# RMSNorm rows by a GpSimd power, a turn in blocks of 32 and a round trip through DRAM, instead of Newton steps and a TensorE broadcast

## The chip, the cores and the metric

The kernel runs on one core of a Trainium2 chip. The metric is device time in microseconds (us) of one execution. Engines: PE is TensorE, DVE is VectorE, ACT is ScalarE, POOL is GpSimd, SP is SyncE, which issues most DMAs. SBUF is the memory on chip with 128 partitions; PSUM, in banks of 128 partitions x 512 numbers, holds what PE sums up.

## The reference

A decoder trunk of two layers on 512 tokens of width 1024, in float32. Layer 0 mixes tokens by multi-head latent attention (MLA), layer 1 by native sparse attention (NSA); each mixer stands between two SwiGLU channel mixers (the ffns) of hidden width 2816. Every one of these six stages starts with an RMSNorm over the width; MLA has two more inside, over the query latent (384) and the key/value latent (256).

```python
def rmsnorm(x, g):
    x32 = x.astype(jnp.float32)
    y = x32 * lax.rsqrt(jnp.mean(x32 * x32, axis=-1, keepdims=True) + RMS_EPS)
    return y.astype(x.dtype) * g

def swiglu(x, w_gate, w_up, w_down):
    return (jax.nn.silu(x @ w_gate) * (x @ w_up)) @ w_down

  h = h + 1/2 * SwiGLU_a(RMSNorm(h))
  h = h + Mixer_i(RMSNorm(h))
  h = h + 1/2 * SwiGLU_b(RMSNorm(h))
```

and one final RMSNorm, which the change does not touch.

## The kernel before

The state h lies in SBUF as eight tiles h0 to h7 of 128 x 512: the width on the partitions, the tokens along the free side. Matrix products run on PE in float32 precision, each as three products of high and low parts (`split` makes the parts: ACT rounds the high part, DVE or POOL subtracts for the low one). Weights come in tile by tile by SP's DMAs and are split in the same way (tiles wr, ru, rg, w, wh, wl).

**A norm is applied late.** The products of a stage run on the tiles of h times the norm's gain, without the factor 1/rms of each token; the results are then multiplied, on DVE, by a tile `row` of 128 x 512 that holds the factor of each token in every partition. So the row is needed only when the first product of a stage leaves PSUM. A row is made in these steps:
1. ACT squares the eight tiles, DVE adds them up (`sumsq`, into s2).
2. `norm_col`: four products of s2 with a column of ones give the sums over the partitions as a column for each block of 128 tokens, a tile `pc` of 128 x 4.
3. `rsqrt` on DVE: v = mean + eps, a first guess by integer operations on the bits (L267, L268), and three Newton steps of three operations (L276, L277, L278), all 128 x 4.
4. `norm_bcast` on PE: four products of the columns, spread over 128, with the identity give `pb`, 128 x 512 in PSUM.
5. ACT copies pb into `row`.

There are seven such rows: in the four ffns (here a0, b0, a1, b1 by layer and place), in MLA for its input (cx) and for the key/value latent (rkv), and in NSA for its input. The query latent's norm in MLA (cq) uses the column alone.

**The head of an ffn.** The hidden width is cut in blocks f of 128. The first two or three blocks are "plain": a product for the gate (pg), a product for the up part (pu), 48 products of 128 x 256 each, with the sums for the norm after block 0 (in a0 the sums come from squares of the tokens, without products). `spread()` then makes the row and applies it: tg<-pg,row (L389), silu, tg<-tg,row (L391), tu<-pu,tg (L400), and the split into ah and al. All later blocks are "fast": seven half-size products (px, pq, pg) of sums of h's quarters and sums of weight quarters. The sums of h are the tiles y, u and four (`combine`), those of the weights s1, rg, ru (`wsums`, L346 to L351), and each weight sum is split into wh and wl ahead of its product.

**MLA's head.** A product pr for the rotary key, then the key/value latent (two tiles pc), the norm cx, the rotary key kr<-pr,row with its small operations (krs on POOL among them), three products for the query latent, the norm rkv, and c<-pc,row (L753), split into four, which the key products pk read.

**NSA's head.** Four products pcm for the compressed keys and values; `layout` multiplies them with the row into tiles xc (L1058, 16 operations); `hidden` is a product ph on xc, a copy posb, a Gelu on ACT; its result hid goes into pkc. `keys(0)` is a product pp (24 matmuls), t<-pp,row and its splits into four; `query` follows.

The program's order on each engine is set by a scheduler from the order of the code; `high_priority(URGENT)` lets what stands inside come earlier. A bank of PSUM or a buffer of a tag is taken again when its last reader is done.

Of the kernel before, what the change touches and what calls it, by code (L numbers as in the profile page):

```python
# [18 lines left out]
P = 128  # L19
S = 512  # L20
# [44 lines left out]
class Kern:  # L65
# [13 lines left out]
    def setup(self):  # L79
# [18 lines left out]
        self.tiny = tiny  # L98

# [160 lines left out]
    def rsqrt(self, y, v, t, psum, n, pool, eps=None):  # L260

        nc = self.nc
        if eps is None:
            nc.vector.tensor_scalar(v, psum, 1.0 / n, EPS, op0=ALU.mult, op1=ALU.add)
        else:
            nc.vector.scalar_tensor_tensor(v, psum, 1.0 / n, eps, op0=ALU.mult, op1=ALU.add)
        nc.vector.tensor_scalar(y.bitcast(I32), v.bitcast(I32), 1, None, op0=ALU.logical_shift_right)  # L267
        nc.vector.tensor_scalar(y.bitcast(I32), y.bitcast(I32), -1.0, float(0x5F3759DF), op0=ALU.mult, op1=ALU.add)  # L268
        for _ in range(3):
            if pool:  # L270
                nc.gpsimd.tensor_tensor(t, y, y, op=ALU.mult)
                nc.gpsimd.tensor_tensor(t, t, v, op=ALU.mult)
                nc.gpsimd.tensor_scalar(t, t, -0.5, 1.5, op0=ALU.mult, op1=ALU.add)
                nc.gpsimd.tensor_tensor(y, y, t, op=ALU.mult)
                continue
            nc.vector.scalar_tensor_tensor(t, y, -0.5, v, op0=ALU.mult, op1=ALU.mult)  # L276
            nc.vector.tensor_tensor(t, t, y, op=ALU.mult)  # L277
            nc.vector.scalar_tensor_tensor(y, t, 1.5, y, op0=ALU.add, op1=ALU.mult)  # L278

    def norm_col(self, n, s2, urgent=0, eps=None):  # L280

        nc = self.nc
        pc = self.bank("o", "pc")
        for i in range(4):
            nc.tensor.matmul(pc[:, i : i + 1], s2[:, i * P : (i + 1) * P], f32v(self.ones)[:, 0:1], start=True, stop=True)
        with self.tc.high_priority(urgent) if urgent else nullcontext():
            return self.rsqrt_col(pc[:, 0:4], n, eps=eps)

    def rsqrt_col(self, s, n, pool=False, eps=None):
        v, t, col = self.vtc[:, 0:4], self.vtc[:, 4:8], self.vtc[:, 8:12]  # L290
        self.rsqrt(col, v, t, s, n, pool, eps)
        return col

    def norm_bcast(self, col):

        pb = self.bank("o", "pb")
        for i in range(4):
            self.nc.tensor.matmul(pb[:, i * P : (i + 1) * P], col[:, i : i + 1].to_broadcast([P, P]), self.ident, start=True, stop=True)
        return pb
# [77 lines left out]
    def ffn(self, idx, gain_next, ap, tp):  # L377
# [63 lines left out]
        def spread():  # L441
            pb = self.norm_bcast(col)
            nc.scalar.activation(row, pb, AF.Copy)
# [4 lines left out]
        row = tp.tile([P, S], F32, tag="row", bufs=1, name="row")  # L448
        gates = [self.bank("T", "pg") for _ in range(plain)]
        for f, g in enumerate(gates):  # L450
            u = tu[f] = self.bank(("mm", "S")[f % 2], "pu")
            self.plain(idx, f, 0, g)
            if f == plain - 1:
                spread()
# [6 lines left out]
            if f == 0 and idx:  # L461
                with self.tc.high_priority(URGENT):
                    for c in self.late:
                        self.sumsq(self.h[c])
                col = self.norm_col(D, self.s2, URGENT)
            elif f == 1 and idx == 0:
                squares(2)
                squares(3)
                col = self.rsqrt_col(sums, D)
# [194 lines left out]
    def mla(self, gain_next):  # L664
        nc, tc, a = self.nc, self.tc, self.a
        with ExitStack() as pools:
# [27 lines left out]
            def rows(col):  # L694
                pb = self.norm_bcast(col)
                t = tp.tile([P, S], F32, tag="o", bufs=12, name="row")
                nc.scalar.activation(t, pb, AF.Copy)
                return t
# [23 lines left out]
            cx = self.norm_col(D, self.s2)  # L722
# [4 lines left out]
            row = rows(cx)  # L727
# [709 lines left out]
```

## Time and profile before

| | |
|---|---|
| time of three runs | 1866.86, 1863.21, 1864.66 us, median 1864.66 |
| span of the profiled execution, first to last instruction | 1860.0 us |
| PE busy | 1841.1 us (99%), 12440 instructions in the trace |
| DVE busy | 1542.0 us (83%), 2862 |
| ACT busy | 1083.9 us (58%), 2044 |
| POOL busy | 232.9 us (13%), 323 |
| granted TensorE clock, mean | 0.999 |
| DMA | 187.44 MB, mean 101 GB/s |

The page gives no time of its own for the profiled execution beside its span; the difference to the runs is what lies before the first instruction and after the last. A row of the timeline gives start, duration, engine, line, operation, output<-input, shapes, count, and in brackets the idle time of the engine just before with what ended it. Rows of PE overlap: what counts is the distance of their starts. A row with a count above one stands for several instructions run together, and a product in float32 is two records of the trace. Lines are those of the kernel before.

### The profile page before, as it was taken

The numbers are of one execution on the slowest core, as the hardware profiler recorded it, in microseconds if no ns is written. First come the engines' busy times: TensorE is split into PE (matmuls) and PEld (weight loads), VectorE is DVE, ScalarE is ACT, GpSimd is POOL, SyncE is SP. The second block draws the span as 40 slices with busy tenths as digits, with TensorE's granted clock in tenths as the row PEclk, the third lists the DMA queues.
The fourth block names the chain that finished last, engine by engine and source line by source line (L and its number), as shares of the span: only waits on it lengthen the run. The fifth ranks groups of instructions, "written<-read, shape, count | busy, mean of one in ns | idle before, by whom it ended". The sixth has DMA issues, their size and how long they took to land. (4 is left out here: it accounts for less than half of the span.)

```text
span 1860.0 us, 32734 instructions
## 1 busy us (share of the span) xinstructions
PE 1841.1 (99%) x12440; PEld 1679.9 (90%) x12440; DVE 1542.0 (83%) x2862; ACT 1083.9 (58%) x2044; POOL 232.9 (13%) x323
## 2 busy tenths in 40 slices
PE   8999999999999999999999999999999999999998
PEld 8999999888889999998999999888888889999997
DVE  8988886688789888887998888765988989988885
ACT  8545554479776554555654545435887866544554
POOL 0000000046500000000000000015666600000000
PEclk9999999999999999999999999999999999999999
DMA  6333333142342333323233332333221124333321
GB/s 245 130 103 102 103 97 115 49 106 72 94 134 94 103 105 112 112 88 115 91 116 110 103 107 87 96 100 97 63 74 63 44 104 131 107 103 106 102 80 67
DMA packets 77901, 187.44 MB, mean 101 GB/s; under 512 B 9632, under 2 KB 37664, under 8 KB 77744
## 3 DMA queue, kind: packets, MB, share of 16 engines
q1 hardware_dynamic: 74640, 180.32, 30.3%
q10 hardware_dynamic: 3104, 5.03, 0.8%
q8 instruction: 98, 1.61, 0.3%
q14 instruction: 59, 0.48, 0.1%
HBM read 178.17 MB, written 2.16 MB: 97 GB/s over the span
## 5 line engine op out<-in xcount | busy, mean ns | idle before, releaser
L167 PE MATMUL pd<-al,wd 128*128 128x512 f32 x576 | 224.1, 389 | 0.0
L168 PE MATMUL pd<-ah,wd 128*128 128x512 f32 x576 | 224.0, 389 | 0.0
L166 PE MATMUL pd<-ah,wd 128*128 128x512 f32 x576 | 224.0, 389 | 0.0
L361 PE MATMUL px<-four,wh 128*128 128x256 f32 x632 | 175.2, 277 | 0.5 <-ACT pg L493 0.5
L363 PE MATMUL px<-four,wl 128*128 128x256 f32 x632 | 174.5, 276 | 0.0
L362 PE MATMUL px<-four,wh 128*128 128x256 f32 x632 | 174.5, 276 | 0.0
L362 PE MATMUL pq<-four,wh 128*128 128x256 f32 x632 | 174.5, 276 | 0.0
L363 PE MATMUL pq<-four,wl 128*128 128x256 f32 x632 | 174.4, 276 | 0.0
L361 PE MATMUL pq<-four,wh 128*128 128x256 f32 x632 | 174.4, 276 | 0.0
L174 ACT ACTIVATE wd<-wdr 128x384 fp32r<-128x384 f32 x192 | 99.2, 519 | 101.5 <-issue 75.5
L175 DVE TENSOR_TENSOR wl<-s,wh 128x512 fp32r<-128x512 f32 x79 | 54.6, 691 | 121.0 <-ACT wh L174 120.9
L413 DVE SCALAR_TENSOR_TENSOR h<-pd,h 128x512 f32<-128x512 f32 x216 | 148.5, 688 | 6.1 <-PE pd L168 6.1
L174 ACT ACTIVATE wh<-s 128x512 fp32r<-128x512 f32 x79 | 49.8, 630 | 136.5 <-PE px L362 131.2
L168 PEld LDWEIGHTS pd<-ah,wd 128*128 128x128 f32 x576 | 108.2, 188 | 22.5
L166 PEld LDWEIGHTS pd<-ah,wd 128*128 128x128 f32 x576 | 108.1, 188 | 19.4
L167 PEld LDWEIGHTS pd<-al,wd 128*128 128x128 f32 x576 | 108.0, 188 | 19.5
L361 PEld LDWEIGHTS px<-four,wh 128*128 128x128 f32 x632 | 118.6, 188 | 1.6 <-ACT pg L493 1.3
L362 PEld LDWEIGHTS px<-four,wh 128*128 128x128 f32 x632 | 118.6, 188 | 0.0
L363 PEld LDWEIGHTS pq<-four,wl 128*128 128x128 f32 x632 | 118.6, 188 | 0.0
L363 PEld LDWEIGHTS px<-four,wl 128*128 128x128 f32 x632 | 118.6, 188 | 0.0
L362 PEld LDWEIGHTS pq<-four,wh 128*128 128x128 f32 x632 | 118.6, 188 | 0.0
L361 PEld LDWEIGHTS pq<-four,wh 128*128 128x128 f32 x632 | 118.6, 188 | 0.0
(367 smaller groups left out, 6037.5 us busy)
## 6 DMA issues: line engine op xcount, KB each, us to landing
wr<-in_w_gu SPq DMA_DIRECT2D x93, 512.0 KB, 3.2
ru<-in_w_gu SPq DMA_DIRECT2D x79, 512.0 KB, 4.2
wdr<-in_w_down SPq DMA_DIRECT2D x192, 192.0 KB, 2.5
wdr<-in_w_down SPq DMA_DIRECT2D x24, 256.0 KB, 2.9
wr<-in_mla_w_o SPq DMA_DIRECT2D x8, 512.0 KB, 3.5
wr<-in_nsa_w_q SPq DMA_DIRECT2D x8, 512.0 KB, 3.5
th<-btab_d SPq DMA_DIRECT2D x16, 256.0 KB, 3.3
wr<-in_nsa_w_o SPq DMA_DIRECT2D x8, 512.0 KB, 3.6
```

The source lines that it names most:

```text
L166: mm(out, wh, xh, start=first, stop=False)
L167: mm(out, wh, xl, start=False, stop=False)
L168: return mm(out, wl, xh, start=False, stop=last)
L174: nc.scalar.activation(hi, src, AF.Copy)
L175: (nc.gpsimd if pool else nc.vector).tensor_tensor(lo, src, f32v(hi), op=ALU.subtract)
L361: mm(out, wh[:, p], xh, start=first and p == 0, stop=False, skip_group_check=True)
L362: mm(out, wh[:, p], xl, start=False, stop=False, skip_group_check=True)
L363: mm(out, wl[:, p], xh, start=False, stop=last and p == KP - 1, skip_group_check=True)
L413: nc.vector.scalar_tensor_tensor(self.h[c], p, 0.5, self.h[c], op0=ALU.mult, op1=ALU.add)
```

## The change

For the seven rows and the cq column, the root is one POOL operation, a power of -0.5 (a constant column `root` is its second operand). For a row it is written into the columns 0, 32, 64, 96 of the row tile, whose first 128 columns POOL has cleared. DVE turns that 128 x 128 in blocks of 32, so that the factors of 32 tokens at a time lie along the free side in partitions 0, 32, 64, 96. A DMA on POOL's queue writes these 16 pieces of 128 bytes to a tile `nrow` in DRAM, and a second one, when the first has landed, reads the 512 numbers into all 128 partitions of the row. The products pb and ACT's copy are gone. In NSA the column stays where it was, since it is used later, and DVE copies it into the row.

Three moves come with it. In ffn b0, a1 and b1 the products for the sums stand between the gate and the up product of block 0, not behind the up product. In MLA `rows` makes column and row in one go: cx's row is started right behind the first latent product, and rkv's ahead of `query_latent(1)`. In NSA the first five pieces of `keys(0)` stand ahead of `hidden(0)`, instead of three behind it.

```diff
+        self.root = self.gains[:, 62:63]
+        nc.gpsimd.memset(self.root, -0.5)
...
-    def rsqrt(self, y, v, t, psum, n, pool, eps=None):
...
-        nc.vector.tensor_scalar(y.bitcast(I32), v.bitcast(I32), 1, None, op0=ALU.logical_shift_right)
-        nc.vector.tensor_scalar(y.bitcast(I32), y.bitcast(I32), -1.0, float(0x5F3759DF), op0=ALU.mult, op1=ALU.add)
-        for _ in range(3):
...
-            nc.vector.scalar_tensor_tensor(t, y, -0.5, v, op0=ALU.mult, op1=ALU.mult)
-            nc.vector.tensor_tensor(t, t, y, op=ALU.mult)
-            nc.vector.scalar_tensor_tensor(y, t, 1.5, y, op0=ALU.add, op1=ALU.mult)
...
+    def rsqrt_col(self, s, n, urgent=0, eps=None, col=None):
+
+        nc, v = self.nc, self.vtc[:, 0:4]
+        col = self.vtc[:, 8:12] if col is None else col
+        with self.urgent(urgent):
...
+                nc.vector.tensor_scalar(v, s, 1.0 / n, EPS, op0=ALU.mult, op1=ALU.add)
...
+        nc.gpsimd.tensor_tensor(col, v, self.root.to_broadcast([P, 4]), op=ALU.pow)
         return col
 
-    def norm_bcast(self, col):
-
-        pb = self.bank("o", "pb")
-        for i in range(4):
-            self.nc.tensor.matmul(pb[:, i * P : (i + 1) * P], col[:, i : i + 1].to_broadcast([P, P]), self.ident, start=True, stop=True)
-        return pb
+    def norm_row(self, row, urgent=0):
+
+        nc = self.nc
+        d = self.dp.tile([4, P], F32, name="nrow")[:, :]
+        with self.urgent(urgent):
+            nc.vector.transpose(row[:, P : 2 * P], row[:, 0:P])
+        nc.gpsimd.dma_start(bass.AP(tensor=d.tensor, offset=d.offset, ap=[[32, 4], [P, 4], [1, 32]]),
+                            row[0:P:32, P : 2 * P].rearrange("g (b c) -> g b c", c=32))
+        nc.gpsimd.dma_start(row, bass.AP(tensor=d.tensor, offset=d.offset, ap=[[0, P], [1, S]]))
+
+    def row_tile(self, pool, **kw):
+        row = pool.tile([P, S], F32, name="row", **kw)
+        self.nc.gpsimd.memset(row[:, 0:P], 0.0)
+        return row
...
         def spread():
-            pb = self.norm_bcast(col)
-            nc.scalar.activation(row, pb, AF.Copy)
...
             self.plain(idx, f, 0, g)
+            if f == 0 and idx:
+                with self.tc.high_priority(URGENT):
+                    for c in self.late:
+                        self.sumsq(self.h[c])
+                self.norm_col(D, self.s2, URGENT, col=row[:, 0:P:32])
+                self.norm_row(row, URGENT)
...
             self.plain(idx, f, 1, u)
-            if f == 0 and idx:
...
-                col = self.norm_col(D, self.s2, URGENT)
-            elif f == 1 and idx == 0:
+            if f == 1 and idx == 0:
                 squares(2)
                 squares(3)
-                col = self.rsqrt_col(sums, D)
+                self.rsqrt_col(sums, D, col=row[:, 0:P:32])
+                self.norm_row(row)
...
-            def rows(col):
-                pb = self.norm_bcast(col)
-                t = tp.tile([P, S], F32, tag="o", bufs=12, name="row")
-                nc.scalar.activation(t, pb, AF.Copy)
+            def rows(n, s2, eps=None):
+                t = self.row_tile(tp, tag="o", bufs=12)
+                self.norm_col(n, s2, URGENT, eps, t[:, 0:P:32])
+                self.norm_row(t, URGENT)
                 return t
...
             ps = [self.proj(a["mla_w_in"][0], P, xh, xl, "pc")]
-            cx = self.norm_col(D, self.s2)
+            row = rows(D, self.s2)
...
             ps.append(self.proj(a["mla_w_in"][1], P, xh, xl, "pc"))
-            row = rows(cx)
...
             query_latent(0)
-            rkv = self.norm_col(KVL, sums[0], eps=eps)
+            rkv = rows(KVL, sums[0], eps)
             query_latent(1)
-            rkv = rows(rkv)
...
                 col = self.norm_col(D, self.s2)
-                nc.scalar.activation(row, self.norm_bcast(col), AF.Copy)
+                nc.vector.tensor_copy(row[:, 0:P:32], col)
+                self.norm_row(row)
                 xc = layout(0, ps)
                 ps = tokens(1)
+                kf = keys(0)
+                for f in kf[:5]:
+                    f()
                 hid, w2 = hidden(0, xc)
-                kf = keys(0)
-                for f in kf[:3]:
-                    f()
```

In the program's order this looks as follows; line numbers of the new kernel are a few lower or higher for the same statement (L389 is L388 there, L175 is L177).

DVE in the head of ffn b0, before: the last Newton step, and what leads to tg<-pg,row and on to the low part of the weight sum rg.

```order
L175 TENSOR_TENSOR wl_6640<-ru_6631,wh_6639 128x1024
L277 TENSOR_TENSOR small_76<-small_76 128x4
L175 TENSOR_TENSOR four_6624<-u_6618,four_6624 128x1024
L278 SCALAR_TENSOR_TENSOR small_76<-small_76 128x4
L351 TENSOR_TENSOR rg_6629<-rg_6629 128x512
L175 TENSOR_TENSOR w_6762<-wr_6757,w_6762 128x1024
L347 TENSOR_TENSOR s1_6761<-ru_6759 128x512
L389 TENSOR_TENSOR tg_6534<-pg_6322,row_6321 128x512
L389 TENSOR_TENSOR tg_6597<-pg_6323,row_6321 128x512
L175 TENSOR_TENSOR wl_6646<-rg_6629,wh_6645 128x1024
```

And with the change, from v to the first tg<-pg,row:

```order
L279 TENSOR_SCALAR small_76<-pc_6343 128x4
L177 TENSOR_TENSOR four_6414<-u_6408,four_6414 128x1024
L290 STREAM_TRANSPOSE row_6279<-row_6279 128x128
L244 TENSOR_TENSOR u_6418<-y_6417,u_6418 128x256
L151 TENSOR_TENSOR w_6429<-wr_6428,w_6429 128x1024
L151 TENSOR_TENSOR w_6492<-wr_6491,w_6492 128x1024
L177 TENSOR_TENSOR four_6424<-u_6418,four_6424 128x1024
L242 TENSOR_TENSOR u_6555<-y_6554 128x512
L242 TENSOR_TENSOR u_6565<-y_6564 128x512
L243 TENSOR_TENSOR u_6555<-y_6554,u_6555 128x256
L388 TENSOR_TENSOR tg_6481<-pg_6281,row_6279 128x512
```

The whole head of the norm has moved ahead of the later sums of h, and with it tg<-pg,row and what follows from it: tg<-tg,row, tu and al of both plain blocks now stand ahead of the low part of rg.

DVE in MLA's head, before, from the last steps of cx to the first operation of rkv's norm:

```order
L277 TENSOR_TENSOR small_76<-small_76 128x4
L278 SCALAR_TENSOR_TENSOR small_76<-small_76 128x4
L258 TENSOR_TENSOR s2_4120<-s2_4120,sq_4159 128x512
L731 TENSOR_TENSOR kr_4162<-pr_4054,row_4157 128x512
L149 TENSOR_TENSOR w_4277<-wr_4276,w_4277 128x1024
L737 TENSOR_TENSOR kr_4162<-kr_4162,kr2_4168 64x512
L266 SCALAR_TENSOR_TENSOR small_76<-pc_4215,small_76 128x4
```

With the change, from cx's v to rkv's turn:

```order
L279 TENSOR_SCALAR small_76<-pc_4093 128x4
L722 TENSOR_SCALAR small_76<-small_76 128x4
L290 STREAM_TRANSPOSE row_4091<-row_4091 128x128
L151 TENSOR_TENSOR w_4208<-wr_4207,w_4208 128x1024
L729 TENSOR_TENSOR kr_4141<-pr_4044,row_4091 128x512
L260 TENSOR_TENSOR s2_4106<-s2_4106,sq_4138 128x512
L735 TENSOR_TENSOR kr_4141<-kr_4141,kr2_4147 64x512
L151 TENSOR_TENSOR w_4245<-wr_4244,w_4245 128x1024
L740 TENSOR_TENSOR kr_4141<-kr_4141,crot_4143 64x512
L742 TENSOR_TENSOR krs_4150<-kr_4141,krs_4150 64x512
L281 SCALAR_TENSOR_TENSOR small_76<-pc_4196,small_76 128x4
L290 STREAM_TRANSPOSE row_4194<-row_4194 128x128
```

One split of a weight stands between cx's turn and kr<-pr,row, and rkv's v has moved behind the whole rotary key.

POOL in the same place, with the change (before, it had only krs and the splits w here):

```order
L297 MEMSET row_4194 128x128
L739 TENSOR_TENSOR krs_4150<-krs_4150,crot_4144 64x512
L282 TENSOR_TENSOR row_4194<-small_76,gains_77 128x4
L291 DMA nrow_4203<-row_4194 4x4x32
L155 TENSOR_TENSOR w_4296<-wr_4295,w_4296 128x512
L293 DMA row_4194<-nrow_4203 128x512
```

The split of a weight (w, 128 x 512) stands between the write and the read of rkv's row.

DVE in NSA's head, before, around the second half of xc and up to the copy posb that the Gelu waits for:

```order
L1058 TENSOR_TENSOR xc_14357<-pcm_14258,row_14123 64x32x8 x4
L149 TENSOR_TENSOR w_14422<-wr_14421,w_14422 128x1024
L1058 TENSOR_TENSOR xc_14357<-pcm_14288,row_14123 64x32x8 x4
L149 TENSOR_TENSOR w_14458<-wr_14457,w_14458 128x1024
L1069 COPY posb_14332<-ph_14315 128x1
```

And with the change:

```order
L1055 TENSOR_TENSOR xc_14297<-pcm_14184,row_14059 64x32x8 x4
L151 TENSOR_TENSOR w_14348<-wr_14347,w_14348 128x1024
L1055 TENSOR_TENSOR xc_14297<-pcm_14214,row_14059 64x32x8 x4
L151 TENSOR_TENSOR w_14384<-wr_14383,w_14384 128x1024
L972 TENSOR_TENSOR t_14269<-pp_14244,row_14059 128x512
L151 TENSOR_TENSOR w_14425<-wr_14424,w_14425 128x912
L980 TENSOR_TENSOR four_14061<-t_14269,four_14061 64x512
L981 TENSOR_TENSOR four_14061<-t_14269,four_14061 64x512
L980 TENSOR_TENSOR four_14061<-t_14269,four_14061 64x512
L1066 COPY posb_14290<-ph_14273 128x1
```

The product pp of `keys(0)` runs on PE ahead of ph now, and t<-pp,row with three of its four low parts stands ahead of posb. On PE pkc has moved behind the first ten of the second ph's sixteen products.

More of the change, by code (lines that the diff above doesn't have):

```diff
@@ L258, in sumsq, with norm_col @@
             nc.vector.tensor_tensor(self.s2, self.s2, sq, op=ALU.add)
-    def rsqrt(self, y, v, t, psum, n, pool, eps=None):
[L262 to L266, printed above, removed]
-        nc.vector.tensor_scalar(y.bitcast(I32), v.bitcast(I32), 1, None, op0=ALU.logical_shift_right)
-        nc.vector.tensor_scalar(y.bitcast(I32), y.bitcast(I32), -1.0, float(0x5F3759DF), op0=ALU.mult, op1=ALU.add)
-        for _ in range(3):
[L270 to L275, printed above, removed]
-            nc.vector.scalar_tensor_tensor(t, y, -0.5, v, op0=ALU.mult, op1=ALU.mult)
-            nc.vector.tensor_tensor(t, t, y, op=ALU.mult)
-            nc.vector.scalar_tensor_tensor(y, t, 1.5, y, op0=ALU.add, op1=ALU.mult)
-    def norm_col(self, n, s2, urgent=0, eps=None):
+    def norm_col(self, n, s2, urgent=0, eps=None, col=None):
         nc = self.nc
@@ L285, in norm_col, with urgent @@
             nc.tensor.matmul(pc[:, i : i + 1], s2[:, i * P : (i + 1) * P], f32v(self.ones)[:, 0:1], start=True, stop=True)
[L286 to L291, printed above, removed]
-        return col
-    def norm_bcast(self, col):
-        pb = self.bank("o", "pb")
-        for i in range(4):
-            self.nc.tensor.matmul(pb[:, i * P : (i + 1) * P], col[:, i : i + 1].to_broadcast([P, P]), self.ident, start=True, stop=True)
-        return pb
+        return self.rsqrt_col(pc[:, 0:4], n, urgent, eps, col)
+    def urgent(self, n):
+        return self.tc.high_priority(n) if n else nullcontext()
+    def rsqrt_col(self, s, n, urgent=0, eps=None, col=None):
+        nc, v = self.nc, self.vtc[:, 0:4]
+        col = self.vtc[:, 8:12] if col is None else col
+        with self.urgent(urgent):
+            if eps is None:
+                nc.vector.tensor_scalar(v, s, 1.0 / n, EPS, op0=ALU.mult, op1=ALU.add)
+            else:
+                nc.vector.scalar_tensor_tensor(v, s, 1.0 / n, eps, op0=ALU.mult, op1=ALU.add)
+        nc.gpsimd.tensor_tensor(col, v, self.root.to_broadcast([P, 4]), op=ALU.pow)
+        return col
+    def norm_row(self, row, urgent=0):
[10 more added lines that the diff above has]
+        return row
     def proj(self, src, m, xh, xl, name, w=None):
@@ L446, in spread @@
                 act(e)
-        row = tp.tile([P, S], F32, tag="row", bufs=1, name="row")
+        row = self.row_tile(tp, tag="row", bufs=1)
         gates = [self.bank("T", "pg") for _ in range(plain)]
@@ L945, in nsa @@
             nc.gpsimd.memset(f32v(kc), 0.0)
-            row = mp.tile([P, S], F32, name="row")
+            row = self.row_tile(mp)
             xh, xl = self.xh, self.xl
@@ L1091, in nsa @@
                 self.split(pk[:, : G * 32].rearrange("p (g n) -> p g n", g=G), at(kch), at(kcl))
-                for f in kf[3:]:
+                for f in kf[5:]:
                     f()
```

3 lines of the change are left out of this document (removed).

## The prediction

> **What bounds the kernel now.** I read the page's first part (busy time), then who PE waits for, and then the timeline of each engine around the eight norms.
>
> ```profile
> PE 1841.1 (99%) x12440; PEld 1679.9 (90%) x12440; DVE 1542.0 (83%) x2862; ACT 1083.9 (58%) x2044; POOL 232.9 (13%) x323
> ```
>
> TensorE (PE) is busy 99% of a span of 1860.0 us. Only two things shorten this kernel: work taken off PE, and the few stretches in which PE waits. POOL is nearly idle. The broadcast that is removed is work on PE, and it costs this much:
>
> ```profile
> 359.62 1.05 PE L298 MATMUL pb<-ident,small 128*128 128x128 f32 x8
> 360.43 0.48 PE L166 MATMUL pc<-x,w 128*128 128x512 f32 x1
> 566.64 1.13 PE L298 MATMUL pb<-ident,small 128*128 128x128 f32 x8 [0.34 <-DVE small L278]
> 567.52 0.36 PE L375 MATMUL pu<-x,w 128*128 128x256 f32 x1
> PE pb L298 <- DVE small L278: 1.0, 3, 0.4
> 395.56 0.44 PE L166 MATMUL s<-four 128*128 128x384 f32 x1 [0.64 <-DVE small L661]
> ```
>
> Start to start, the four products pb hold PE 0.81 us in MLA and 0.88 us in ffn b0. Seven of them make about 6.0 us. The waits ahead of pb for the last Newton step (L278) are 1.0 us in three places (total, count, longest), and the wait for the first softmax, which stands behind the Newton steps of the cq norm on VectorE (DVE), is 0.64 us. So the ceiling of the whole change is 6.0 + 1.0 + 0.6 = 7.6 us, 0.4% of the time.
>
> **What the new path costs.** v goes to POOL for the power, back to DVE for the turn in blocks of 32, to POOL's queue for the write, and, when that has landed, for the read. The power is 128x4; the nearest POOL row is the small one below, so 0.2 us, and I take 0.4 with the hand-overs (bounds 0.2 and the 1.34 us of POOL's 128x512). The turn is 128x128 on DVE; its neighbours are the 128x4 rows of 0.16 us and the 128x256 rows of 0.42 (both quoted with the heads below), the bounds, and I take 0.3 between them. With v's own 0.16 and a hand-over the turn ends v + 0.95 us when DVE is free.
>
> ```profile
> L920 POOL TENSOR_SCALAR btab<-tb 16x2 f32<-16x2 f32 x1 | 0.2, 185 | 0.0
> L153 POOL TENSOR_TENSOR w<-wr,w 128x512 fp32r<-128x512 f32 x43 | 56.8, 1340 | 56.7 <-ACT w L147 56.3
> four<-in_g_fin ACTq DMA_DIRECT2D x2, 256.0 KB, 3.3
> rot<-in_c_rope ACTq DMA_DIRECT2D x2, 256.0 KB, 2.6
> tb<-in_rel_bias ACTq DMA_DIRECT2D x1, 2.0 KB, 1.5
> btab_d<-btab ACTq DMA_DIRECT2D x1, 65.0 KB, 4.7
> pos<-in_nsa_pos ACTq DMA_DIRECT2D x2, 8.0 KB, 4.9
> ```
>
> The trace has no DMA of POOL's queue, so the time L from the end of the turn to the landed row is bounded. The read has a twin: four<-in_g_fin spreads one row of 512 numbers over 128 partitions, 3.3 us from issue to landing. It could be as short as rot's 2.6 or as long as the 4.9 of pos. The write is 2 KB: 1.5 us as tb, the same bytes the other way, or 4.7 as btab_d, a write of 65 KB; I take 2.2, near tb by size, more because it writes to DRAM. With 0.5 for two issues and hand-overs L is 2.2 + 3.3 + 0.5 = 6.0 us, from 4.1 to 9.6. L decides the sign, as follows.
>
> **The four ffn heads.** In b0, a1 and b1 the sums move ahead of the up product of block 0, 48 products sooner, and v with them. The row, used at 568.90 before, would land near 559. But tg<-pg,row also moves forward on DVE: behind the turn stand only one L244, two L151, one L177, two L242 and one L243 before it.
>
> ```profile
> 552.85 1.22 DVE L175 TENSOR_TENSOR four<-u,four 128x1024 fp32r<-128x1024 f32 x1
> 553.99 0.42 DVE L242 TENSOR_TENSOR u<-y,u 128x256 f32<-128x256 f32 x1
> 554.32 1.22 DVE L149 TENSOR_TENSOR w<-wr,w 128x1024 fp32r<-128x1024 f32 x1
> 555.46 0.69 DVE L240 TENSOR_TENSOR u<-y 128x512 f32<-128x512 f32 x1
> 556.06 1.22 DVE L175 TENSOR_TENSOR four<-u,four 128x1024 fp32r<-128x1024 f32 x1
> 557.53 0.16 DVE L264 TENSOR_SCALAR small<-pc 128x4 f32<-128x4 f32 x1
> 568.90 1.29 DVE L389 TENSOR_TENSOR tg<-pg,row 128x512 f32<-128x512 f32 x2
> 570.11 1.22 DVE L175 TENSOR_TENSOR wl<-rg,wh 128x1024 fp32r<-128x1024 f32 x1
> 569.80 0.28 PE L361 MATMUL px<-x,w 128*128 128x256 f32 x1
> 571.16 0.28 PE L361 MATMUL pq<-four,wh 128*128 128x256 f32 x1
> 572.78 0.28 PE L363 MATMUL px<-four,wl 128*128 128x256 f32 x1
> ```
>
> The first five rows follow each other without a gap, so DVE is full here, and they give the prices start to start: 1.14 us for 1024 columns, 0.60 for 512, 0.33 for 256. PE's products of 256 columns go one in 0.113 us (twelve between the first two PE rows), so the 48 are 5.4 us. The work before tg is 3 x 1.14 + 2 x 0.60 + 2 x 0.33 = 5.3 us. At L = 6.0 DVE stands 0.7 us at tg, and all its list behind it shifts. That list feeds PE: the low part wl<-rg, done before at 571.33, for the px at 572.78. In the new order two tg*row, two tu and two al come ahead of it, 6 x 0.60 = 3.6 us; one s1 goes behind it (-0.6); eleven tiny operations of 0.16 like the L264 row vanish, of which I count half, since neighbours overlap (bounds 0 and 1.8), -0.9; the turn adds 0.25. It ends at 571.33 + 2.35 + 0.7 = 574.4. On PE fifteen more products of 0.11 stand before that px now, while pb and its gap are gone: 572.78 + 1.7 - 0.9 - 0.3 = 573.3. PE waits 1.1 us where it saved 1.2: net -0.1. Each us of L is a us here, down to -0.8 at L = 5.3, where the wait at tg is gone. I take -0.1 for a1 and b1 too, whose heads are alike, and for a0, whose sums stay but whose tg stands 5.7 us behind the turn. Four heads: -0.4. The POOL clearing of the row's first columns has no producer and costs nothing while POOL is idle.
>
> **MLA.**
>
> ```profile
> 354.27 0.16 DVE L264 TENSOR_SCALAR small<-pc 128x4 f32<-128x4 f32 x1 [3.92 <-PE pc L285]
> 361.34 0.69 DVE L731 TENSOR_TENSOR kr<-pr,row 128x512 f32<-128x512 f32 x1 [0.20 <-ACT row L697]
> 366.97 0.16 DVE L266 SCALAR_TENSOR_TENSOR small<-pc,small 128x4 f32<-128x4 f32 x1 [2.82 <-PE pc L285]
> 367.96 1.76 POOL L153 TENSOR_TENSOR w<-wr,w 128x512 fp32r<-128x512 f32 x1 [1.15 <-ACT w L147]
> 374.54 1.28 DVE L753 TENSOR_TENSOR c<-pc,row 128x512 f32<-128x512 f32 x2
> 376.02 1.42 DVE L178 SCALAR_TENSOR_TENSOR four<-c,gains,four 128x512 fp32r<-128x512 f32 x2 [0.20 <-ACT four L177]
> 378.81 0.39 PE L166 MATMUL pk<-four,w 128*128 128x512 f32 x1
> ```
>
> The first row lands at 354.27 + 0.95 + 6.0 = 361.2, as it did (kr at 361.34). The sum for rkv comes 0.8 sooner with one pb gone, v near 366.2, the second row near 373.3 with POOL's own delay, and c (row L753, 374.54 before) about 1.2 sooner, so four ends near 376.2 instead of 377.44. PE reaches the keys' first pk at 378.81 - 1.6 = 377.2. The two pbs are gained whole, and I add half of the 0.64 at the first softmax: -1.9. POOL's 128x512 w stands between write and read of the second row, 1.76 us, beside the write. Beyond L = 6.4 both rows delay the keys, the second waiting for DVE's kr list behind the first: 2 us for each us of L.
>
> **NSA.** Here the column is wanted again later, so it is copied into the row first (one more DVE operation, 0.2, and the turn at v + 1.3).
>
> ```profile
> 1228.76 0.16 DVE L264 TENSOR_SCALAR small<-pc 128x4 f32<-128x4 f32 x1 [1.41 <-PE pc L285]
> 1234.07 7.66 DVE L1058 TENSOR_TENSOR xc<-pcm,row 64x256 f32<-64x256 f32 x12 [1.94 <-ACT row L1080]
> 1243.01 2.55 DVE L1058 TENSOR_TENSOR xc<-pcm,row 64x256 f32<-64x256 f32 x4
> 1242.04 1.28 ACT L1073 ACT_TABLE_LOAD   x1
> 1251.67 0.61 ACT L981 ACTIVATE four<-t 64x512 fp32r<-64x512 f32 x1
> 1247.51 0.46 PE L1089 MATMUL pkc<-hid,w 128*128 128x128 f32 x2 [0.24 <-issue]
> 1250.55 3.74 PE L1067 MATMUL ph<-xc,w 128*128 128x129 f32 x32
> 1254.04 0.48 PE L166 MATMUL pp<-x,w 128*128 128x512 f32 x1
> ```
>
> DVE already idles 1.94 us for the row and starts xc at 1234.07. The new row lands at 1228.76 + 1.3 + 6.0 = 1236.1, 2.0 later, and xc is one solid list. The reorder puts t<-pp and the hi/lo splits ahead of posb and hid. From the row: sixteen xc 10.2, two w 2.4, t 0.7, four splits on ACT 2.5, the table load 1.3, hid and hand-over 0.6, so pkc can run 17.7 us after the row, at 1253.8. Behind pkc PE keeps only six ph (sixteen in 1250.55 to 1254.04, so 1.3 in all) and pkc's own 0.2; it would reach pkc at 1254.04 - 1.5 - 0.9 (pb) - 0.2 (the gap ahead of pkc) = 1251.4, and waits 2.4. Net 2.4 - 0.9 - 0.2 = +1.3, a us for a us of L.
>
> **The sum** at L = 6.0 is -0.4 - 1.9 + 1.3 = -1.0 us. The profiled execution spans 1860.0 and the median of the three runs is 1864.66, so 4.7 us lie around the span (the runs spread from 1863.21 to 1866.86). 1859.0 + 4.7 gives 1863.7. The slope is 5 us for each us of L up to 6.4 and 7 beyond.
>
> **The rivals.** *Faster, 0.34: the landings are short.* Below L = 5.5, between tb's 1.5 + rot's 2.6 = 4.1 and my value, the waits at tg vanish: heads 4 x -0.8, MLA -1.9, NSA about 0 gives -5.1 and 1859.6; the ceiling, 7.6, gives 1857.1. For it speaks that tb's size and pieces are those of the write. Against it: the only write in the trace took 4.7. [...]
>
> *Slower, 0.28: POOL's three steps (power, two issues) each wait for a running DVE operation.* In the heads DVE has no gap, and its operations last up to 1.22 us; POOL's 128x512 rows average 1.34 us, and the one quoted in MLA lasted 1.76. Three waits of half such an operation add 1.8 and make L 7.8: 0.4 x 5 + 1.4 x 7 = 11.8 over my sum, 1875.5. It decides from L = 6.8, where the loss passes 3.7 us; the place where it bites first is the keys in MLA. A write as long as btab_d's would do the same. [...]
>
> *Same within 0.2%, 0.38: L between 5.5 and 6.8*, 1861 to 1868. 0.2%, or 3.7 us, is about what this measurement can tell from no change. In this case belongs that the heads gain nothing because DVE's list, not the row, is what PE waits for.
>
> The forecast is the middle case. The range takes in the short landings nearly to the ceiling and the long ones to L = 7.4 (-1.0 + 2 + 7 = +8): 1857.5 to 1872. Cases of both signs hold most of the chance; the middle one's own range is 1861 to 1868.
>
> **What would show it.** No pb, no row copy on ACT, and PE busy about 6 us less. The two nrow DMAs' landings add up to 5.5 us without issue. In b0 DVE stops below 1 us at tg for the row's DMA; px<-four waits about 1 us for wl. In MLA pk has no wait. In NSA DVE waits at xc about 4 us, and pkc waits 2 to 3 us. I am wrong if a write or read lands after 4 us or more, if POOL's power takes above 1 us, or if tg is reached late enough to hide all of L.

## The result, and the profile after

The changed kernel takes 1887.81 us (median of 4 runs, 1885.33 to 1889.96) against 1864.1 us before: 1.0128 times as long, 95% interval 1.0116 to 1.0141, or 23.7 us slower. The forecast was 1863.7, in a range of 1857.5 to 1872.0.

The profiled execution spans 1888.1 us against 1860.0, so it is 28.1 us longer, more than the 23.7 of the medians: at 1889.96 us it lies 2.2 above the median of its kernel. Numbers by place below are from it. Its busy times, its new DMA queue, and whom PE waits for (line, releaser, total us, times, longest):

```profile
PE 1851.2 (98%) x12384; PEld 1684.7 (89%) x12384; DVE 1536.5 (81%) x2782; ACT 1080.8 (57%) x2037; POOL 253.7 (13%) x353
q0 software_dynamic: 784, 1.85, 0.3%
PE pq L362 <- DVE wl L177: 5.4, 3, 2.4
PE pkc L1087 <- issue: 3.8, 1, 3.8
PE pk L168 <- ACT four L179: 2.8, 1, 2.8
PE pu L374 <- DVE w L151: 1.7, 1, 1.7
```

PE has 56 records fewer, the seven broadcasts, and is busy 10 us more. Part of the answer stands in the granted clock, the share of full speed that the trace records for TensorE. These are windows of 16 and 24 us in MLA's keys and ffn b0, of before and then of the changed kernel (busy us of PE, of the weight load, DVE, ACT and POOL, each with its count; then the granted clock, the DMA share, GB/s):

```profile
376.00:392.00 16.00, 16.00 (x77) 13.35 (x76) 11.42 (x22) 9.82 (x18) 6.02 (x5) 1.00 0.35 98
572.00:596.00 24.00, 24.00 (x182) 22.81 (x182) 24.00 (x38) 14.86 (x26) 0.00 (x0) 1.00 0.35 119
```
```profile
376.00:392.00 16.00, 13.24 (x45) 10.04 (x44) 10.65 (x12) 6.89 (x12) 4.08 (x5) 0.79 0.42 116
572.00:596.00 24.00, 20.65 (x145) 19.50 (x145) 21.15 (x31) 12.16 (x20) 0.00 (x0) 0.86 0.19 66
```

After the waits the clock is at half for a while. The trace's clock record has four such stretches inside the changed program, 6.83, 6.83, 3.41 and 6.83 us (MLA, b0, NSA, b1), and none before. In MLA it looks like this on PE's timeline:

```profile
384.06 0.79 PE L168 MATMUL pk<-four,w 128*128 128x512 f32 x1 [2.75 <-ACT four L179]
386.71 0.63 PE L170 MATMUL pk<-four,w 128*128 128x512 f32 x1
387.14 0.63 PE L168 MATMUL pk<-four,w 128*128 128x512 f32 x1
```

The products start 0.43 us apart, where the same shape starts every 0.23 us at full clock in the trace of before (378.81, 379.04).

The chain of a row, on POOL and in the list of DMAs (KB and us to landing), in a0, MLA and b0, and then on DVE, in b0, a0 and NSA:

```profile
31.50 0.59 POOL L293 DMA_DIRECT2D row<-nrow  x1 [3.77 <-DMA nrow<-row]
358.88 1.05 POOL L282 TENSOR_TENSOR row<-small,gains 128x4 f32<-128x4 f32 x1 [10.25 <-DVE small L279]
360.58 0.64 POOL L291 DMA_DIRECT2D nrow<-row  x1 [0.64 <-DVE row L290]
362.88 0.57 POOL L293 DMA_DIRECT2D row<-nrow  x1 [1.66 <-DMA nrow<-row]
559.63 1.87 POOL L282 TENSOR_TENSOR row<-small,gains 128x4 f32<-128x4 f32 x1 [29.74 <-DVE small L279]
nrow<-row POOLq DMA_DIRECT2D x7, 2.0 KB, 1.7
row<-nrow POOLq DMA_DIRECT2D x7, 256.0 KB, 4.2
```
```profile
559.32 0.16 DVE L279 TENSOR_SCALAR small<-pc 128x4 f32<-128x4 f32 x1
561.54 0.31 DVE L290 STREAM_TRANSPOSE row<-row 128x128 f32<-128x128 f32 x1 [0.93 <-POOL row L282]
569.64 0.69 DVE L388 TENSOR_TENSOR tg<-pg,row 128x512 f32<-128x512 f32 x1 [2.54 <-DMA row<-nrow]
590.16 1.23 DVE L177 TENSOR_TENSOR wl<-ru,wh 128x1024 fp32r<-128x1024 f32 x1 [1.86 <-ACT wh L176]
593.06 0.69 DVE L388 TENSOR_TENSOR tg<-pg,row 128x512 f32<-128x512 f32 x1 [0.99 <-PE pg L362]
35.70 1.29 DVE L388 TENSOR_TENSOR tg<-pg,row 128x512 f32<-128x512 f32 x2 [3.90 <-DMA row<-nrow]
1252.53 0.63 DVE L1055 TENSOR_TENSOR xc<-pcm,row 64x256 f32<-64x256 f32 x1 [5.46 <-DMA row<-nrow]
```

The power takes 1.05 to 1.9 us. From the end of the turn it is 0.3 us to the write's issue, 1.7 to 1.8 to its landing (4.0 in a0), 0.5 to 0.7 to the read's issue and 4.2 (3.6 to 5.2) to the landed row: 6.8 in all with the middle values, 9.1 in a0, and in b0 10.3 us from v to tg (559.32 to 569.64). DVE, which had no gap in b0's head before, stands 0.93, 2.54, 1.86 and 0.99 us.

What TensorE waits for in b0 is not the row itself but the low part of a weight sum, wl<-ru, which the products pq read. Before, it was done 6 us ahead of them, and ahead of both tg; now it stands behind two tg<-pg,row, two tg<-tg,row, one tu and one al, and every stand of DVE ahead of it delays it. DVE and PE, before and then with the change:

```profile
563.99 1.22 DVE L175 TENSOR_TENSOR wl<-ru,wh 128x1024 fp32r<-128x1024 f32 x1
571.38 0.28 PE L363 MATMUL pq<-four,wl 128*128 128x256 f32 x1
```
```profile
578.26 1.22 DVE L177 TENSOR_TENSOR wl<-ru,wh 128x1024 fp32r<-128x1024 f32 x1
579.53 0.39 PE L362 MATMUL pq<-four,wl 128*128 128x256 f32 x1 [2.22 <-DVE wl L177]
```

Where the loss lies, from equal PE products in the two traces: a0 +4.2, MLA +3.0, b0 +6.2, a1 +1.5, NSA +4.5, b1 +8.3, 27.7 us in all. Such distances are given by place for the other kernels too.

### The profile page after: what moved, and what is told of

It reads as the page before. It is cut to its first block, busy times and chain, and to the rows that moved or that the text cites. A ratio compares the mean times of both kernels' runs of the same rounds, so it can differ in the third digit from the quotient of the medians.

```text
span 1888.1 us, 32584 instructions
## 1 busy us (share of the span) xinstructions
PE 1851.2 (98%) x12384; PEld 1684.7 (89%) x12384; DVE 1536.5 (81%) x2782; ACT 1080.8 (57%) x2037; POOL 253.7 (13%) x353
## 5 line engine op out<-in xcount | busy, mean ns | idle before, releaser
L177 DVE TENSOR_TENSOR wl<-s,wh 128x512 fp32r<-128x512 f32 x79 | 54.5, 689 | 119.3 <-ACT wh L176 119.3
```

Source lines behind the costliest of these rows:

```text
L177: (nc.gpsimd if pool else nc.vector).tensor_tensor(lo, src, f32v(hi), op=ALU.subtract)
```

## The experiments

The first theory was lateness: the row comes too late, and the clock makes each wait dearer. Its rival was order: the moves put the norm's work ahead of what TensorE needs.

**The power alone**, in place of the root from bits and three Newton steps on DVE.

```diff
-        nc.vector.tensor_scalar(y.bitcast(I32), v.bitcast(I32), 1, None, op0=ALU.logical_shift_right)
...
+        nc.gpsimd.tensor_tensor(y, v, self.root.to_broadcast([P, 4]), op=ALU.pow)
```

> The kernel before with one change: the root by GpSimd's power in place of the bit operations and Newton steps; broadcast by TensorE, row copy by ACT and all places as before. Latency theory (the loss of the changed kernel comes from the time from v to the landed row, and from the TensorE clock that halves after the waits): the power takes 1.05 to 1.9 us in the trace of the changed kernel, the eleven small DVE operations it replaces took 2.2 us back to back and 9 us in the full heads, so the waits ahead of pb (1.0 us) and part of that ahead of the first softmax (0.6) go: 1 to 2 us faster, 1862.5 to 1863.7. Rival, the power itself is what hurts (POOL in the chain, locked out by DVE): slower by 2 us or more, with longer waits ahead of pb.

1864.87 us, ratio 1.0007 (0.9999 to 1.0016): no change. MLA is 1.0 ahead, b0 0.9, but NSA 1.4 behind: its broadcast waits 1.9 us for the power. The small gain that was expected is not there, and neither is harm of 2 us or more from the power by itself.

**The moves alone**, with Newton roots, broadcast and row copy: the sums half a block sooner, and in NSA five keys ahead of hidden(0), where three stood behind it.

```diff
             self.plain(idx, f, 0, g)
+            if f == 0 and idx:
...
+                col = self.norm_col(D, self.s2, URGENT)
...
-                hid, w2 = hidden(0, xc)
...
-                for f in kf[:3]:
+                for f in kf[:5]:
...
+                hid, w2 = hidden(0, xc)
```

> The kernel before with the moves alone: the sums of ffn b0, a1, b1 ahead of block 0's up product, and five pieces of keys(0) ahead of hidden(0) in NSA; roots, broadcast and row copy as before. Latency theory: the row is there sooner, nothing waits for it, so 1862 to 1866, no half clock inside the program. Rival, the order does it (tg, tu and al ahead of the low parts that TensorE needs, posb behind the key splits): the waits for wl in b0, a1, b1 and for pkc stay, slower by 8 to 20 us, 1873 to 1885.

1863.8 us, ratio 1.0001 (0.9992 to 1.001). The moves by themselves cost nothing. DVE's list is not that of the changed kernel here, since the Newton steps stand in it; the next run has that list.

**Rows without lateness.** The row is loaded early from 512 numbers of a weight, so the norm's factor is left out of the results; the power, a turn and a small write go on beside it.

```diff
+        g = self.a["w_last"]
+        self.nc.gpsimd.dma_start(row, bass.AP(tensor=g.tensor, offset=g.offset, ap=[[0, P], [1, S]]))
```

> The changed kernel with all its moves, but the row tile is loaded early from 512 numbers of a weight, so that nothing waits for the norm; the power, a turn of 128x32 and a write of 4 pieces go on beside it without a reader, and the norm's factor is left out of the results. Latency theory: all waits of the changed kernel go and the seven broadcasts are gone, 5 to 8 us faster than before, 1857 to 1860, and the clock is never halved inside the program. Rival, the order does it: the waits for wl and pkc stay, 1870 or more.

1863.62 us, ratio 1.0001 (0.9992 to 1.001). In b0 the same twenty operations stand between the turn and wl<-ru as in the changed kernel, so it is not their order that costs: lateness is the loss. But the forecast gain of 5 to 8 us is not there either. By place: MLA -3.0 and NSA -1.7, where broadcasts really were on the path; b0 +1.2, a1 +0.3, b1 +0.9; a0 +3.1. What a0 loses here lies in the first 20 us and belongs to the stand-in: the first products wait 1.6 us for a tile of h, whose loads land after 7.1 us (median) beside the first row load instead of 4.9, and the clock reaches full speed at 14.8 us instead of 10.0. The places without a0 add up to 2.3 us ahead. With free rows the heads of b0, a1 and b1 gain nothing from the missing broadcasts. In b0 DVE is full but for 0.94 us, in which it still stands for the power ahead of the turn, and PE's one longer wait, 1.4 us at px, is for a copy of ACT's that stands behind ACT's split of rg, the last of DVE's sums.

**Idle products in PE's waits**, in the heads ahead of the last product of pq, in MLA ahead of the keys, in NSA ahead of pkc.

```diff
+                self.fill(10)
             self.product(7, w, q, True, False)
...
+            self.fill(12)
...
+                self.fill(26)
```

> The changed kernel with idle TensorE work where TensorE waits: products of the identity with itself that nobody reads, 12 ahead of the keys in MLA, 10 ahead of the first pq of the low parts in ffn b0 and b1, 26 ahead of pkc in NSA, 58 in all, 11.7 us at the 0.2 us of a broadcast product. If the halved clock after a wait is a cost of its own: the fill takes the place of the waits, the four windows of half clock (6.8, 6.8, 3.4 and 6.8 us in the changed kernel's trace, half of which is lost) go, and the kernel is 8 to 12 us faster than the changed one, 1876 to 1880, with more work. If the clock is a bystander, the time stays that of the changed kernel, 1887, or grows by what the fill doesn't hide, to 1892.

1888.92 us, ratio 1.0136 (1.0122 to 1.015): no gain over the changed kernel, where 8 to 12 us were expected. By place MLA went from +3.0 to +0.05, as expected: its fill took the wait, and the clock stayed at full in the window of MLA's keys,

```profile
376.00:392.00 16.00, 15.85 (x86) 13.44 (x85) 13.61 (x16) 9.37 (x17) 6.95 (x8) 1.00 0.42 118
```

but b0 stayed at +6.1 and b1 at +8.1: PE got through its fill and waited 1.7 and 1.7 us at the next two products for wh and wl instead. In NSA the fill pushed the second ph behind pkc, +4.9.

**More fill in b0 and b1**, 14 products more ahead of the px that waits next, none in NSA.

> The changed kernel with idle TensorE products at more of its waits: 12 ahead of the keys in MLA; in ffn b0 and b1 10 ahead of the first pq of the low parts and 14 ahead of the px that waits for wh and wl after it. NSA has none. The first fill took the half clock out of MLA (3.0 us gained in the trace there) but left b0 and b1 where they were, since there the wait only moved on to px. If the halved clock is a cost of its own: MLA is at +0, b0 and b1 at +3 to +4 instead of +6.2 and +8.3 in the trace, 6 to 9 us less than the changed kernel, 1879 to 1882. If in the heads DVE's list sets the end and TensorE's clock is a bystander there: MLA alone gains, 1885 to 1888.

1889.65 us, ratio 1.0139 (1.0122 to 1.0156), a little above the 1885 to 1888 of the second case. MLA -0.1; b0 +7.5 and b1 +7.8, without any stretch of half clock in either. So the full clock alone did not bring the heads back. What the half clock costs there this run can't tell, since the fill is itself longer (4.9 us) than the waits that it fills (3.3).

**The same DMAs from another queue.**

```diff
-        nc.gpsimd.dma_start(row, bass.AP(tensor=d.tensor, offset=d.offset, ap=[[0, P], [1, S]]))
+        nc.scalar.dma_start(row, bass.AP(tensor=d.tensor, offset=d.offset, ap=[[0, P], [1, S]]))
```

The write is moved likewise; in the second kernel both stand on `nc.sync`.

> The changed kernel, its two DMAs of each row issued on ACT's queue. In the changed kernel a row took, from the end of the turn, 0.3 us to the issue, 1.75 to the write's landing, 0.5 to the read's issue and 4.2 to its landing, 6.8 in all. Theory, POOL's queue makes the round trip long: the read lands in 3.3 us as the same spread does from ACT's queue before the change and the hand-overs shrink, 5.5 us in all; 1.3 us less in each of seven rows, and fewer half-clock windows, 6 to 12 us faster than the changed kernel: 1876 to 1882. Rival, the trip is as long from any queue: 1886 to 1890, or more, since ACT's work behind the waiting DMAs (four, y, wh) is late too.

> As the one before, on SP's queue, where no work of ACT stands behind the waits, only weight loads. Theory, POOL's queue makes it long: 1874 to 1882. Rival, the trip is as long from any queue: 1886 to 1890; if weight loads that stand ahead wait for buffers, the rows are later still, above 1890.

From ACT's queue 1870.36 us, ratio 1.0039 (1.0025 to 1.0053); from SP's 1874.47, ratio 1.0056 (1.0041 to 1.0071). So up to 17 of the 24 us went with POOL's queue, more than expected. The trip from turn to use is 5.2 to 6.5 us outside a0 on both queues. In b0 DVE's timeline reads, on ACT's queue and then on SP's,

```profile
554.09 0.31 DVE L290 STREAM_TRANSPOSE row<-row 128x128 f32<-128x128 f32 x1 [0.93 <-POOL row L282]
560.83 0.69 DVE L388 TENSOR_TENSOR tg<-pg,row 128x512 f32<-128x512 f32 x1 [0.57 <-DMA row<-nrow]
552.03 0.31 DVE L290 STREAM_TRANSPOSE row<-row 128x128 f32<-128x128 f32 x1 [0.92 <-POOL row L282]
558.60 0.69 DVE L388 TENSOR_TENSOR tg<-pg,row 128x512 f32<-128x512 f32 x1 [0.33 <-DMA row<-nrow]
```

1.4 us less of trip took 2.0 us from DVE's wait at tg and 4.4 us from b0 (+6.2 to +1.8); the halved clock is gone with it, and of the later stands of 1.86 and 0.99 us one of 0.43 is left. On ACT's queue the scheduler has also put wl<-ru ahead of tg<-tg,row, so that run changes two things. SP's run changes one: the same twenty operations stand ahead of wl<-ru as in the changed kernel, the trip is 1.5 us shorter, and b0 is at +1.5. MLA is at -2.15 on ACT's queue and -1.9 on SP's, a gain at last. On SP's queue NSA is at +6.7: its pkc waited 5.2 us.

**MLA and NSA alone**, heads with power and broadcast, POOL's queue.

> The changed path in MLA (two rows) and NSA (one row); the four ffn heads with the sums where they were, the root by power, the broadcast by TensorE and ACT's copy. By place the changed kernel's trace is later than before by 4.2 us in a0, 3.0 in MLA, 6.2 in b0, 1.5 in a1, 4.5 in NSA and 8.3 in b1. If the places add up: about 7.5 us slower than before, 1869 to 1873, so that two thirds of the loss lie in the heads. Rival, the loss is that of MLA and NSA and spreads (buffers, weight loads): 1880 or more.

1870.52 us, ratio 1.004 (1.0026 to 1.0054), inside the 1869 to 1873 that were expected if the places add up. The profiled execution is the fastest of the five, 1867.57 us, and in it MLA alone is not as expected: it is at +0.2, with a wait of 2.1 us at pk and no half clock, against +3.0 with 2.75 us and 6.8 us of half clock in the changed kernel. The wait itself only gives back what the broadcasts had cost; of the 2.8 us between the two, 0.6 is the longer wait, and the rest is within the 3.4 us, half of 6.8, that this half clock can cost by estimate.

**The pieces on an idle chip.**

> None of the trunk: only the pieces of the new path on an idle chip, one after the other. A power of 128x4 on POOL and, for comparison, a product of 128x4, each four times alone, beside a DVE operation with two SBUF inputs (128x1024), beside one with a PSUM and an SBUF input (128x512), and beside one with a single input (128x1024); then the write of 16 pieces and the read back over 128 partitions, three times from each of POOL's, ACT's and SP's queue. Theory, the power is slow by itself and DVE's two-input operations hold it up: 1.05 us alone and 1.5 to 2.1 beside the two-input operation, a product 0.2 us alone; the trip from the write's issue to the landed row 6.5 to 7 us from POOL and 5 to 5.5 from ACT and SP. Rival, the long powers and trips come from the load of the full program (weight loads, TensorE): the power takes one time in all four settings, and all three queues need the same time.

```profile
nrow<-row POOLq DMA_DIRECT2D x3, 2.0 KB, 1.7
row<-nrow POOLq DMA_DIRECT2D x3, 256.0 KB, 3.6
row<-nrow ACTq DMA_DIRECT2D x3, 256.0 KB, 3.0
row<-nrow SPq DMA_DIRECT2D x3, 256.0 KB, 3.0
```

From one issue of the write to the next, with one DVE operation between, the trips are 6.3 us apart from POOL and 5.0 to 5.4 from ACT and SP, so 1 us of the difference is POOL's own even without load. The power took 1.01 to 1.03 us in every setting and a product of the same size 0.20. The DVE operation chosen had a column operand and did not hold it up. So the next one used the subtraction of the splits:

> None of the trunk: again the power and a product of 128x4 on POOL on an idle chip, each four times alone and beside DVE operations of the forms that the heads use: a subtraction of two SBUF inputs into float32 (128x1024), the same into the rounded type of the splits, a subtraction of a PSUM and an SBUF input (128x512), and for comparison the operation with a column operand that did not slow the power in the last run. In the heads the power took 1.87 to 1.94 us where such a split ran and 1.05 where DVE stood. Theory, the two-input subtraction holds POOL up: 1.5 to 2.2 us beside it, 1.0 alone. Rival, something else of the full program does: 1.0 in all settings.

POOL's timeline, the power alone, beside a subtraction of two SBUF tiles, beside the same with a PSUM tile, beside the operation with a column; then a product alone and beside the subtraction:

```profile
9.48 1.01 POOL L1358 TENSOR_TENSOR small<-big,small 128x4 f32<-128x4 f32 x1 [0.28 <-DVE big L1357]
10.76 2.05 POOL L1358 TENSOR_TENSOR small<-big,small 128x4 f32<-128x4 f32 x1 [0.28 <-DVE big L1357]
29.40 1.01 POOL L1358 TENSOR_TENSOR small<-big,small 128x4 f32<-128x4 f32 x1 [0.28 <-DVE big L1357]
36.19 1.01 POOL L1358 TENSOR_TENSOR small<-big,small 128x4 f32<-128x4 f32 x1 [0.62 <-DVE big L1357]
42.52 0.20 POOL L1358 TENSOR_TENSOR small<-big,small 128x4 f32<-128x4 f32 x1 [0.28 <-DVE big L1357]
43.00 1.24 POOL L1358 TENSOR_TENSOR small<-big,small 128x4 f32<-128x4 f32 x1 [0.28 <-DVE big L1357]
```

Beside the subtraction of two SBUF tiles, which lasts 1.23 us, POOL's operation took 1.04 us longer, a power (2.05 against 1.01) as well as a product (1.24 against 0.20); beside the other two forms it took no longer than alone (1.01). The 1.87 in b0, where four<-u,four (L177) starts behind v, against 1.05 in MLA agrees with that.

**Less DVE work behind the wait.**

```diff
+            if pool is self.wp and idx and f < PLAIN[idx] + 3:
+                nc.scalar.activation(hi, src, AF.Copy)
+                nc.scalar.activation(lo, src, AF.Copy)
```

> The changed kernel with less DVE work in the heads of b0, a1 and b1: the low parts of the first three fast blocks' plain weights (w<-rg, w<-wr, 128x1024, 1.14 us of DVE each) are written by ACT as copies of the weights; the subtraction is left out there, so these products are not the reference's. Theory, in the heads DVE's list sets the end, and a stand of DVE for the row is paid in full: with 1.1 to 2.3 us of DVE work gone behind tg<-pg,row, b0 and b1 are at +2 to +4 instead of +6.2 and +8.3 in the trace and a1 at or below +1; 1878 to 1883. Rival, TensorE's halved clock and the wait itself set the end there: the same 1886 to 1889.

1880.25 us, ratio 1.0093 (1.0077 to 1.011). b0 +2.6 and b1 +2.5 instead of +6.2 and +8.3, although DVE still stood 2.6 and 2.5 us at tg, PE still waited 2.4 and 2.3 us at pq, and a stretch of 3.4 us of half clock came in both. That stretch is half as long as the 6.8 us of the changed kernel, which is worth at most 1.7 us. By this estimate at least 1.9 us in b0 and 4.1 in b1 came with the shorter list, so in these two heads DVE's list bounds PE. In a1 the expectation failed: +3.1 instead of +1.5, with new waits of 1.9 and 1.7 us at px for copies out of PSUM by ACT, which had the more work.

**A version from the gains.** MLA's rows through DRAM on ACT's queue, its three roots by power, everything else as before; then NSA's move as well.

> The kernel before with MLA's two rows through DRAM, on ACT's queue, and MLA's three roots by power; heads and NSA as before. By the trace of the version on ACT's queue MLA is 2.15 us ahead of before there, the only place that gains. If the places add up: 2 us faster than before, 1861.5 to 1862.5, ratio 0.9989. Rival, a small change in MLA is lost in what follows: ratio 1.000.

> The one before and NSA's move (five pieces of keys(0) ahead of hidden(0)), with NSA's root and row as before; in the run of the moves alone NSA was 0.5 us ahead. If the places add up: 2.5 us faster than before, ratio 0.9986; rival: no difference from the one before.

1862.22 us, ratio 0.9995 (0.9986 to 1.0004), and 1861.52, ratio 0.9988 (0.9979 to 0.9997). That is 1.0 and 1.7 us by the medians, where 2 and 2.5 were expected. In the traces MLA is 2.2 and 2.5 us ahead, and b0 gives 1.4 and 1.0 back. The first can't be told from no change. The second is the fastest seen here, by about 0.1%, and its interval barely leaves 1.

## Why the prediction was wrong

Two steps failed: the length of the chain from v to the row, and what a us of it costs.

**The ceiling** of 7.6 us for the removed broadcasts was out of reach. I added up PE's time for seven of them and the waits ahead. With rows that cost no waiting, only MLA and NSA gained (3.0 and 1.7); in the heads the time of the broadcast had also been time for DVE's list, and without it PE waits for that list.

**The power** was the first mis-sized term: 0.4 us with hand-overs from a 16x2 row, measured 1.05 alone and 1.87 beside a split, and about 0.2 of hand-overs more. The turn ended 1.7 to 2.5 us behind v instead of 0.95. The bounds of the power were 0.2 and 1.34, and in b0 and b1 it broke the upper one. Its own DVE stand of 0.93 us ahead of the turn was not in the sum at all.

**L**, the trip, was put at 6.0 and was 6.5 to 7.9 outside a0 and 9.1 in a0, within the bounds of 4.1 to 9.6. Outside a0 the write was over-sized (2.2, measured 1.7), the read under-sized (3.3 from ACT's twin, measured 4.2 from POOL's queue), and the hand-overs were 0.8 to 1.0 instead of 0.5. Both errors together make the chain from v to row 1.0 to 3.5 us longer than forecast, 3.8 in a0. Two of the signs that the prediction named for being wrong came true: every power took over 1 us, and six of the seven reads landed after 4 us or more.

**The price of a us** was the second step. The sum lets every us of the chain count once, in one place. Put into that account, the measured chains give some +15 us (an estimate: a0 +3.7, MLA +0.9, b0 +3.3, a1 +1.5, NSA +2.3, b1 +3.4); measured are 27.7. The difference lies almost wholly in the four places with a half clock: MLA 2.1, b0 2.9, NSA 2.2, b1 4.9, against 0.5 in a0 and none in a1. Between POOL's and ACT's queue it is 17 us for some 1.4 us of trip, 12 per us instead of 5 to 7, DVE's other order included. In b0 DVE's wait at tg came back in full, and again as two stands of 1.86 and 0.99 us after PE's clock had halved; in MLA a wait of 2.1 us without a half clock left +0.2 in the run of MLA and NSA alone, and one of 2.75 us with 6.8 us of half clock behind it +3.0 in the changed kernel. The trace of before had no such wait (0.64 us was the longest behind the start), its clock was 1.00 in all these places, and I read it as a constant.

**By place.** b0 was to lose 1 us per us of L from -0.1; it lost 6.2. The prediction looked for PE's wait at px, 1.1 us for wl<-rg; it came one product earlier, 2.2 us at pq for wl<-ru, which the reckoning had not followed. a0, put at -0.1, lost 4.2: its write landed after 4.0 us, DVE stood 3.9 us at tg, and PE waited 1.7 us at pu, 0.7 at px and 0.9 at pq. The 0.9 us for eleven vanished small operations was mostly not there: DVE's busy time in b0 fell by 0.3 (99.3 to 99.0). a1, taken as b0's like, lost only 1.5: DVE had only a short operation behind v there (u<-y,u, 0.41 us), the power took 1.08 us, tg was reached with 1.2 us of wait, and the clock did not halve. MLA's account was right in its parts: it gave a gain of 1.9 as long as L stays under 6.4, and -2.15 was measured from ACT's queue, where the trip is that short; from POOL's queue L was beyond that point and the keys waited, as it said. What it lacked was the clock behind that wait. NSA's waits were of the right kind and under-sized: DVE was to wait about 4 us at xc and pkc 2 to 3; measured 5.5 and 3.8.

**Small slips.** The 4.7 us around the span are not all outside the program: every timed execution on record lasts 1.7 to 2.2 us longer than its span, so the rest is that the profiled execution of before was faster than the median. And the upper end of the range, worked out at L = 7.4, is 1872.7 rather than 1872. Neither touches the outcome.

**The rivals.** What the slower rival supposed was seen for the power alone: it took 2.05 us beside a DVE subtraction of two SBUF tiles and 1.01 alone. Two SBUF inputs by themselves did not do it: the operation with a column operand also reads two SBUF tiles, and beside it the power took 1.01. It is not what made the DMAs long: their issue took 0.64 us with DVE busy (b0's write) and 0.60 to 0.75 on the idle chip, and the write landed after 1.7 us in both, a0 left aside. The faster rival's read of 2.6 us, rot's, was too short: POOL's read took 3.6 on the idle chip and 4.2 in the program.

What stays open: the price of the halved clock in the heads, where the fills did not isolate it from DVE's list; why the write takes 4.0 us in a0; what decides whether the clock halves behind a wait, beyond the one trace below; and why POOL's read lands 0.6 us later than ACT's of the same bytes on an idle chip.

## What to carry to other kernels

Work on the bound engine that covers another engine's list is not a gain when it goes: look, place by place, which engine has no gap. The round trip through DRAM as a broadcast gained more than half a us in one place only, MLA, and there only from ACT's or SP's queue. Before a small operation moves to POOL, see which DVE operations run beside it: beside the subtraction of two SBUF tiles the power here took 2.05 us instead of 1.01. And look at the clock behind every wait of TensorE: behind the four of 2.2 to 3.8 us in the changed kernel it was at half for 3.4 to 6.8 us, an estimated 1.7 to 3.4 us each at most.

## What the runs showed of the hardware that I had not expected

On the idle chip a POOL power of 128x4 took 1.01 us, five times the 0.20 of a product of the same size. Beside a DVE subtraction of two SBUF tiles of 128x1024 the power took 2.05 us and the product 1.24, each 1.04 more; beside one with a PSUM tile and beside the operation with a column operand they took 1.01 and 0.20, as alone.

In the changed kernel's trace the clock halves four times inside the program, at 383.56, 581.53, 1271.02 and 1561.16 us, for 6.83, 6.83, 3.41 and 6.83 us, 2.2 to 4.4 us behind the start of a wait of PE (2.75, 2.22, 3.79 and 2.41 us, its only waits over 2 us behind the start of the program). The length of a wait alone doesn't decide it: a wait of 2.13 us in MLA, in the run of MLA and NSA alone, was not followed by a half clock, nor was one of 3.79 us in NSA in the kernel with less DVE work. In the changed kernel's trace all these changes of the clock, down and up, lie a whole number of steps of 3.413 us apart (2, 56, 2, 200, 1, 84 and 2 steps from one to the next). With the trace cut into windows at these steps and PE's idle time added up in each, PE stood 2.26, 2.00, 2.82 and 2.34 us in the four windows that end where the clock halves, and at most 1.74 us (35.40 to 38.81) in any other between the first full clock at 11.5 us and the last products. In the first window at half clock PE stood 0.50, 0.53 and 0.95 us in MLA, b0 and b1, where a second one followed, and 0.00 in NSA, where none did. This is one trace, and that it holds for others was not shown. First the window ahead of MLA's half clock in the changed kernel, then the 3.79 us wait of NSA there, of which 0.97 us lie in one window and 2.82 in the next, with the half clock behind it, then the 3.79 us wait of NSA in the kernel with less DVE work, with 1.9 us of idle PE in each of two windows and no half clock behind it:

```profile
380.15:383.56 3.41, 1.15 (x6) 0.61 (x4) 1.51 (x3) 0.28 (x1) 0.00 (x0) 1.00 1.01 242
1264.20:1267.61 3.41, 2.45 (x20) 2.25 (x20) 3.38 (x4) 2.45 (x4) 0.00 (x0) 1.00 0.37 94
1267.61:1271.02 3.41, 0.58 (x5) 0.62 (x6) 2.18 (x5) 2.76 (x5) 0.00 (x0) 1.00 0.44 138
1260.46:1263.87 3.41, 1.50 (x14) 1.31 (x12) 3.33 (x6) 2.97 (x5) 0.00 (x0) 1.00 0.56 153
1263.87:1267.28 3.41, 1.53 (x14) 1.56 (x15) 1.57 (x4) 2.03 (x4) 0.00 (x0) 1.00 0.26 83
```

So a wait of the same 3.79 us was followed by a half clock in the one trace and not in the other. Seven executions of the kernel on ACT's queue had mean clocks from 0.999 to 0.995 and took 1868.4 to 1877.5 us.
